# One byte offset and one run length for split weights: the up projection at 192 and 64, the queries and keys at 0 and 8 in runs of sixteen

## The chip, the cores and the metric

The kernel runs on one core of one Trainium2 chip. Five engines with a queue each matter here: TensorE (PE, with its weight loads as PEld), VectorE (DVE), ScalarE (ACT), GpSimd (POOL) and SyncE (SP), whose queue issues the transfers. An engine takes its instructions in the order in which they stand in its queue. The metric is the device time of one execution in microseconds; for a kernel it is the median of its runs.

## The reference

One conditioned decoder layer over 256 tokens of width 2048, in float32, and a last RMSNorm:

```
mod = silu(c) W_ada + b_ada
h   = RMSNorm(x)(1+scale1)+shift1
p   = h W_in        # retention q,k,v,g | HGRN2 q,f,i,g | gates A, B
yA  = W_retO( LN_head(Retention(rope(q),rope(k),v)) * silu(g) )
yB  = W_hgO( RMS_head(HGRN2(silu(q), f, i)) * silu(g) )
x   = x + gate1 * ( (sigmoid(gA)*yA + sigmoid(gB)*yB) W_out )
h2  = RMSNorm(x)(1+scale2)+shift2
u   = causal_depthwise_conv3(h2 W_up) ; [a, b] = split(u)
x   = x + gate2 * ( (silu(a) * b) W_down )
out = RMSNorm_final(x)
```

W_up is 2048 x 11264, W_down 5632 x 2048. The weights are the bulk of the work: each is read once.

## The kernel before

**Split products.** Each product with a weight is made of three: the weight is split into an upper part `wh` (an ACT copy to the type fp32r, L180) and a lower part `wl` (DVE: weight minus `wh`, L185), and the activations likewise into a left and a right half of one tile. With `n` = 256 tokens, an upper part meets both halves and a lower part meets the left one only. Where the weight is the stationary operand, an upper matmul moves 512 columns (both halves at once) and a lower matmul 256; an upper and a lower of one weight block go to the same bank of PSUM.

**Rings.** A weight piece of 128 x 2 x 512 is loaded by SP into a ring of 11 buffers (`raw`), split into a ring of 4 buffers for `wh` and one of 4 for `wl`. `part` (L168 to L171) gives each of these four buffers 64 elements more than a piece needs and lays the piece at a byte offset, the `shift`, inside it. A shift changes the address of the stationary operand and nothing else.

**Stages in order of time.**

1. 16 to 288 us: the input projection's first groups. Four of them (HGRN2's f and q) keep the weight stationary (`mm_cols`, 256 columns a matmul, L225 and L226 upper, L229 lower); after their first pieces these groups are visited in turn, a few row tiles at a time, with the shifts of the group's row in `COLS`; the first pieces have no shift. The others (`mm_rows`, L209, L210, L214) keep the activations stationary.
2. 288 to 387 us: four groups of queries and keys for the retention (`wide_group`). A group has 4 column tiles z, 16 row tiles kt, and 4 steps of 4 row tiles. Each step runs for z = 0, 1 and then for z = 2, 3 (`pair`): 8 upper matmuls (L236), then 8 lower (L239). The first pair sums into the two banks of one PSUM buffer, the second pair into those of another; there are two such buffers (`pg`), and the next group uses the same two. At the end ACT copies the right halves of a buffer to SBUF (L257) and DVE adds the left halves (L258), buffer by buffer. Between the steps the chunk work of HGRN2 is issued (`pump`): scores (L615, L663), the output matmuls `po<-p,at` and `po<-p,a` (L722, L724), their head norm (squares `sqh` L728 and `rsh` L321 on ACT, reciprocal L322 and `oh` L732 on DVE), and the gate f (sigmoid L576, bounds L581 on ACT).
3. 387 to 764 us: gates, values and the output projections by rows.
4. 774 to 1259 us: 22 up groups (`up_group`), 4 column tiles and 16 row tiles each. A step has two row tiles, 8 upper matmuls (L1144) and 8 lower (L1146). `UPS` gives every group a run length and two shifts: with 8 the uppers of a step go first and then its lowers, with 16 two steps are joined, with 2 two uppers and two lowers alternate. Groups alternate between `pg` and four `po` banks, so a group's sums have the length of a group to be emptied.
5. 1259 to 1498 us: the down projection by rows.

**What sets the order.** Instructions that are pinned (`pin`) keep the program's order; the others are placed by a scheduler that looks at engines and buffers. `pump` spends a rate on the work in the background, so a step's `pump` decides at which step the HGRN2 pieces are offered to it.

## Time and profile before

| | us |
|---|---|
| median of 3 runs | 1507.48 |
| lowest and highest | 1507.36, 1507.76 |
| the profiled execution | 1507.86 |
| its span | 1506.0 |
| PE busy | 1489.8 |
| DVE busy | 1207.3 |
| ACT busy | 839.6 |

The profile is of one execution. Its span is the time from the first to the last instruction recorded, 1.9 us less than that execution's own time. A row of a timeline gives the start, the length, the engine, the line of the kernel, the operation, the tiles (out<-in, without buffer numbers), the size, and how many instructions the row joins; in square brackets stands the idle time of the engine just before, and what ended it. Matmuls overlap: the next one starts before the last has ended, so the pace of PE is read from start to start and not from the length of one. Windows give the busy time of each engine in a stretch, and in the column PEclk the clock that PE was granted (1.00 is full).

### The profile page before, as it was taken

The page shows a single profiled execution, that of the slowest core. Times are in us where ns is not written, and L with a number is a line of the kernel's source. Part 1 is how long each engine was busy: PE and PEld are TensorE (multiplying, and loading weights), DVE is VectorE, ACT ScalarE, POOL GpSimd, SP SyncE. Part 2 cuts the span into 40 slices and gives each one's busy share as a digit, 9 for nine tenths or more (in the row PEclk, how much of TensorE's full clock was granted, in tenths as well). Part 3 has the DMA queues.
Part 4 walks back from the last instruction along what each step waited for, and adds up shares of the span by engine and source line. Part 5 has one row for each costly group of instructions (what it writes and reads, how often), then busy time and mean ns, then how long its engine had stood idle before and what let it go on. Part 6 is the DMA issues. An engine that isn't in the chain of part 4 may idle for free.

```text
span 1506.0 us, 22669 instructions
## 1 busy us (share of the span) xinstructions
PE 1489.8 (99%) x8466; PEld 1273.8 (85%) x8466; DVE 1207.3 (80%) x1647; ACT 839.6 (56%) x1210; POOL 4.0 (0%) x8
## 2 busy tenths in 40 slices
PE   8999999999999999999999999999999999999997
PEld 6889899888888888888888888888888888888886
DVE  7899997998999877898977778777777769455694
ACT  5745456767775644455466555545555558344342
POOL 0000000000000000000000000000000000000000
PEclk9999999999999999999999999999999999999999
DMA  9999997878787899989847777777677766667651
GB/s 374 360 340 345 313 335 255 265 253 278 279 277 263 283 302 325 316 292 358 304 129 239 243 231 236 225 238 233 215 248 228 228 188 209 197 207 212 179 186 56
DMA packets 110995, 385.71 MB, mean 256 GB/s; under 512 B 12803, under 2 KB 13347, under 8 KB 110885
## 3 DMA queue, kind: packets, MB, share of 16 engines
q1 hardware_dynamic: 110016, 383.14, 76.7%
q8 instruction: 66, 1.08, 0.3%
q10 hardware_dynamic: 868, 1.13, 0.2%
q14 instruction: 45, 0.36, 0.1%
HBM read 382.11 MB, written 2.11 MB: 255 GB/s over the span
## 4 chain that ended last, share of the span: by engine, by line
PE 94%; DVE 2%; ACT 2%; DMA 1%; issue 1%; SPq 0%; DVEq 0%; ACTq 0%
PE pg L209 13%; PE pg L210 13%; PE pg L214 13%; PE po L1144 11%; PE pg L1144 10%; PE po L1146 5%; PE pg L1146 5%; PE pg L236 4%; PE po L214 3%; PE po L209 3%; PE po L210 3%; PE pg L239 2%; PE pg L229 1%; PE pg L226 1%; PE pg L225 1%; DVE raw L469 1%
## 5 line engine op out<-in xcount | busy, mean ns | idle before, releaser
L185 DVE TENSOR_TENSOR wl<-raw,wh 128x1024 fp32r<-128x1024 f32 (+1 forms) x536 | 631.1, 1189 | 232.6 <-ACT wh L180 194.6
L180 ACT ACTIVATE wh<-raw 128x1024 fp32r<-128x1024 f32 (+1 forms) x536 | 547.3, 1032 | 472.5 <-PE pg L210 198.1
L469 DVE SCALAR_TENSOR_TENSOR raw<-raw,sc 128x1024 f32<-128x1024 f32 x192 | 233.3, 1219 | 0.0
L209 PE MATMUL pg<-wh,hT 128*128 128x512 f32 x512 | 202.2, 395 | 0.7 <-ACT wh L180 0.6
L210 PE MATMUL pg<-wh,hT 128*128 128x512 f32 x512 | 199.8, 390 | 0.0
L1144 PE MATMUL po<-h2T,wh 128*128 128x512 f32 x704 | 178.2, 392 | 0.0
L1144 PE MATMUL pg<-h2T,wh 128*128 128x512 f32 x688 | 173.9, 393 | 0.0
L1144 PEld LDWEIGHTS po<-h2T,wh 128*128 128x128 f32 x704 | 125.0, 188 | 21.3
L1144 PEld LDWEIGHTS pg<-h2T,wh 128*128 128x128 f32 x688 | 122.7, 188 | 21.5
L214 PE MATMUL pg<-wl,hT 128*128 128x512 f32 x512 | 138.4, 390 | 0.1
L209 PEld LDWEIGHTS pg<-wh,hT 128*128 128x128 f32 x512 | 96.1, 188 | 21.1 <-ACT f L590 1.0
L214 PEld LDWEIGHTS pg<-wl,hT 128*128 128x128 f32 x512 | 96.0, 188 | 20.6 <-DVE wl L185 0.4
L210 PEld LDWEIGHTS pg<-wh,hT 128*128 128x128 f32 x512 | 96.2, 188 | 19.6 <-DVE hT L398 0.3
L1146 PEld LDWEIGHTS po<-h2T,wl 128*128 128x128 f32 x704 | 96.3, 188 | 8.5
L1146 PEld LDWEIGHTS pg<-h2T,wl 128*128 128x128 f32 x688 | 93.2, 188 | 8.4 <-DVE wl L185 0.6
L1146 PE MATMUL po<-h2T,wl 128*128 128x256 f32 x704 | 98.2, 279 | 0.0
L1146 PE MATMUL pg<-h2T,wl 128*128 128x256 f32 x688 | 95.3, 279 | 0.1
L210 PE MATMUL pg<-wh,gs 128*128 128x512 f32 x176 | 68.6, 390 | 0.0
L209 PE MATMUL pg<-wh,gs 128*128 128x512 f32 x176 | 68.5, 389 | 0.0
L209 PE MATMUL po<-wh,gs 128*128 128x512 f32 x176 | 68.5, 389 | 0.0
L210 PE MATMUL po<-wh,gs 128*128 128x512 f32 x176 | 68.5, 389 | 0.0
L1157 ACT ACTIVATE u<-uy,convw 128x256 f32<-128x256 f32 x88 | 52.3, 594 | 27.3 <-DVE uy L1155 27.0
(255 smaller groups left out, 2027.9 us busy)
## 6 DMA issues: line engine op xcount, KB each, us to landing
raw<-in_wup SPq DMA_DIRECT2D x176, 512.0 KB, 4.6
raw<-in_wdown SPq DMA_DIRECT2D x88, 512.0 KB, 4.0
raw<-in_wa SPq DMA_DIRECT2D x80, 512.0 KB, 5.7
raw<-in_ada SPq DMA_DIRECT2D x64, 512.5 KB, 5.7
raw<-in_ada SPq DMA_DIRECT2D x64, 512.0 KB, 5.5
raw<-in_wab SPq DMA_DIRECT2D x64, 512.0 KB, 5.2
raw<-in_gate SPq DMA_DIRECT2D x32, 512.5 KB, 5.0
raw<-in_wk SPq DMA_DIRECT2D x32, 512.0 KB, 5.2
```

What stands on the lines that cost most here:

```text
L180: self.pin(self.nc.scalar.activation(wh, raw, AF.Copy))
L185: self.last = self.nc.vector.tensor_tensor(wl, raw, wh.bitcast(F32), ALU.subtract)
L209: nc.tensor.matmul(ps[t], lhsT=act[:, hi], rhs=wh, start=first and i == 0, stop=False)
L210: nc.tensor.matmul(ps[t], lhsT=act[:, lo], rhs=wh, start=False, stop=False)
L214: nc.tensor.matmul(ps[t], lhsT=act[:, hi], rhs=wl, start=False, stop=last and i == len(items) - 1)
L225: nc.tensor.matmul(outs[j], lhsT=wh[:, cs[j]], rhs=act[:, :T], start=opens, stop=False, skip_group_check=True)
L236: nc.tensor.matmul(ps[z], lhsT=wh[:, z * P : (z + 1) * P], rhs=act, start=first and i == 0, stop=False)
L239: nc.tensor.matmul(ps[z][:, :T], lhsT=wl[:, z * P : (z + 1) * P], rhs=act[:, :T], start=False, stop=last and i == len(items) - 1)
L469: dot = self.pin(nc.vector.scalar_tensor_tensor(raw[:, 0, :], raw[:, 0, :], 1.0, self.sc[:, u * GW : u * GW + w], ALU.mult, ALU.mult, accu ...
L1144: self.pin(nc.tensor.matmul(ps[z], lhsT=wh[:, z * P : (z + 1) * P], rhs=act, start=kt == 0, stop=False, skip_group_check=bool(begun)))
L1146: nc.tensor.matmul(ps[z][:, :T], lhsT=wl[:, z * P : (z + 1) * P], rhs=act[:, :T], start=False, stop=kt == KT - 1, skip_group_check=bool(be ...
L1157: nc.scalar.activation(u, y, AF.Identity, bias=w[3], scale=w[2])
```

## The change

The tables go. All four visited column groups take shift 8; before, the third had 72 and the fourth 4. All up groups take runs of eight with the uppers at 192 and the lowers at 64, which two of the 22 groups had before (the second and the nineteenth). The queries and keys take 0 for the uppers and 8 for the lowers (before, (0, 64) and (192, 192) in turn), and a step no longer runs pair by pair: it runs 16 uppers for z = 0 to 3 and then 16 lowers, and offers the background work of two pumps at once behind them. `shift` is now a row of four numbers, two for each of two pieces in turn.

```diff
-UPS = (
-    (2, 192, 192), (8, 192, 64), (8, 192, 192), (16, 144, 64), (8, 192, 8), (8, 192, 208), (8, 192, 176), (8, 192, 0),
-    (8, 192, 224), (8, 176, 64), (8, 208, 64), (8, 200, 64), (8, 184, 64), (8, 224, 64), (16, 144, 8), (16, 144, 192),
-    (16, 192, 8), (16, 144, 0), (8, 192, 64), (8, 192, 192), (16, 144, 64), (2, 192, 192),
-)
-WIDES = ((0, 64), (192, 192), (0, 64), (192, 192))
-COLS = ((8, 8), (8, 8), (72, 72), (4, 4))
+COLS = (8,) * 4
+WIDE = (0, 8, 0, 8)
+UP = (192, 64, 192, 64)
...
-                uppers.append(self.upper(src[:, at : at + z, :], z, G, gain, shift))
+                uppers.append(self.upper(src[:, at : at + z, :], z, G, gain, shift[at % 4 : at % 4 + 2]))
...
-    def mm_wide(self, ps, items, first, last, pair):
+    def mm_wide(self, ps, items, first, last):
 
         nc = self.nc
         for i, (act, wh, _) in enumerate(items):
-            for z in (pair, pair + 1):
+            for z in range(4):
                 nc.tensor.matmul(ps[z], lhsT=wh[:, z * P : (z + 1) * P], rhs=act, start=first and i == 0, stop=False)
         for i, (act, _, wl) in enumerate(items):
-            for z in (pair, pair + 1):
+            for z in range(4):
                 nc.tensor.matmul(ps[z][:, :T], lhsT=wl[:, z * P : (z + 1) * P], rhs=act[:, :T], start=False, stop=last and i == len(items) - 1)
 
-    def wide_group(self, src, act, shift=(0, 0)):
+    def wide_group(self, src, act):
...
-        pieces = self.pieces(src, KT, shift=shift)
+        pieces = self.pieces(src, KT, shift=WIDE)
         for k in steps:
             items = [(act(kt), wh, wl) for _ in range(2) for kt, wh, wl in next(pieces)]
-            for pair in (0, 2):
-                self.mm_wide(ps, items, k == 0, k == steps[-1], pair)
-                self.pump()
+            self.mm_wide(ps, items, k == 0, k == steps[-1])
+            self.pump(2)
...
-            return COLS[cols.index(g)] if g in cols else (0, 0)
+            return COLS if g in cols else (0,) * 4
...
-        run = UPS[i][0]
         for step in pieces:
-            step = list(step)
-            if run == 16 and not begun:
-                step += next(pieces)
             some = [(kt, act2(kt), wh, wl, z) for kt, wh, wl in step for z in range(4)]
-            for at in range(0, len(some), run):
-                part = some[at : at + run]
-                for kt, act, wh, wl, z in part:
-                    self.pin(nc.tensor.matmul(ps[z], lhsT=wh[:, z * P : (z + 1) * P], rhs=act, start=kt == 0, stop=False, skip_group_check=bool(begun)))
-                for kt, act, wh, wl, z in part:
-                    nc.tensor.matmul(ps[z][:, :T], lhsT=wl[:, z * P : (z + 1) * P], rhs=act[:, :T], start=False, stop=kt == KT - 1, skip_group_check=bool(begun))
+            for kt, act, wh, wl, z in some:
+                self.pin(nc.tensor.matmul(ps[z], lhsT=wh[:, z * P : (z + 1) * P], rhs=act, start=kt == 0, stop=False, skip_group_check=bool(begun)))
+            for kt, act, wh, wl, z in some:
+                nc.tensor.matmul(ps[z][:, :T], lhsT=wl[:, z * P : (z + 1) * P], rhs=act[:, :T], start=False, stop=kt == KT - 1, skip_group_check=bool(begun))
             self.pump(len(step) / 2)
```

The number of matmuls and of transfers stays. In the stage of the queries and keys the scheduler places the HGRN2 work differently. The lines of the kernel after stand four to ten lower: the upper matmuls of this stage are L232, the lowers L235, the copy L252, the addition L253.

The first place is on PE, in the third of these groups, around its last step but one. `pg_3519` and `pg_3520` are the group's two buffers, `po_3712` (`po_3693` before) and `po_3730` hold the HGRN2 outputs. Before:

```order
L722 MATMUL po_3693<-p_133,at_3020 128x128 x4
L236 MATMUL pg_3520<-hT_1331,wh_3666 128x512 x4
L236 MATMUL pg_3520<-hT_1658,wh_3672 128x512 x4
L239 MATMUL pg_3520<-hT_1331,wl_3667 128x256 x4
L239 MATMUL pg_3520<-hT_1658,wl_3673 128x256 x4
L722 MATMUL po_3730<-p_133,at_3020 128x128
L724 MATMUL po_3730<-p_133,a_465_3083 128x128
```

And after the change:

```order
L235 MATMUL pg_3520<-hT_1658,wl_3673 128x256 x2
L717 MATMUL po_3712<-p_133,at_3036 128x128 x4
L717 MATMUL po_3730<-p_133,at_3036 128x128
L719 MATMUL po_3730<-p_133,a_465_3099 128x128
L717 MATMUL po_3730<-p_133,at_3036 128x128
```

The four products into `po` that stood between the two pairs of a step now stand behind the whole step, directly ahead of the eight others; after these the group's last step follows in both kernels.

The second place is on ACT, where the copies out of the same group's buffers stand (`p_3805<-pg_3519` and `pg_3520`). Before:

```order
L321 ACT_TABLE_LOAD
L321 ACTIVATE rsh_3704<-ssh_3698,eps_73 128x4
L728 ACTIVATE sqh_3740,ssh_3739<-po_3730 128x128 x4
L490 ACTIVATE gate_2905<-dot_3781 128x1
L321 ACTIVATE rsh_3745<-ssh_3739,eps_73 128x4
L576 ACT_TABLE_LOAD
L576 ACTIVATE f_3785<-p_130 128x1024
L257 ACTIVATE p_3805<-pg_3519 128x512
L581 ACTIVATE f_3785<-f_3785,lb,lb_1687 128x256
L257 ACTIVATE p_3805<-pg_3520 128x512
```

And after the change:

```order
L723 ACTIVATE sqh_3740,ssh_3739<-po_3730 128x128
L571 ACT_TABLE_LOAD
L571 ACTIVATE f_3801<-p_130 128x1024
L723 ACTIVATE sqh_3740,ssh_3739<-po_3730 128x128
L576 ACTIVATE f_3801<-f_3801,lb,lb_1687 128x256
L723 ACTIVATE sqh_3740,ssh_3739<-po_3730 128x128
L576 ACTIVATE f_3801<-f_3801,lb,lb_1687 128x256
L316 ACT_TABLE_LOAD
L316 ACTIVATE rsh_3745<-ssh_3739,eps_73 128x4
L252 ACTIVATE p_3805<-pg_3519 128x512
L252 ACTIVATE p_3805<-pg_3520 128x512
```

The sigmoid of f now stands among the squares instead of behind the second `rsh`, and a table load stands ahead of that `rsh`. The first four squares, another table load and the first `rsh` stand ahead of these rows after the change too: from the first square to the first copy there are three table loads after the change and two before it.

The third place is on DVE, at the end of the fourth group (buffers `pg_3810` and `pg_3811`), where the stage passes into the products by rows. Before:

```order
L185 TENSOR_TENSOR wl_4033<-raw_4030,wh_4032 128x1024
L469 SCALAR_TENSOR_TENSOR raw_4050,dot_4049<-raw_4050,sc 128x1024
L185 TENSOR_TENSOR wl_4058<-raw_4055,wh_4057 128x1024
L609 TENSOR_TENSOR ke_4075<-b_3787 128x512
L258 TENSOR_TENSOR p_4023<-p_4023,pg_3810 128x512
```

And after the change:

```order
L181 TENSOR_TENSOR wl_4058<-raw_4055,wh_4057 128x1024
L181 TENSOR_TENSOR wl_4085<-raw_4082,wh_4084 128x1024
L464 SCALAR_TENSOR_TENSOR raw_4100,dot_4049<-raw_4100,sc 128x1025
L253 TENSOR_TENSOR p_4023<-p_4023,pg_3810 128x512
L253 TENSOR_TENSOR p_4023<-p_4023,pg_3811 128x512
```

The addition out of the first buffer now stands behind one lower split more, that of the third piece of the rows, and behind the dot that follows it; the addition out of the second buffer follows at once.

## The prediction

> **What bounds the kernel now.** I read the page first, then the busy time by stage, then the timeline of each engine at the places where the change acts. The page's head, its line of busy time and the chain of waits by engine:

> ```profile
> span 1506.0 us, 22669 instructions
> PE 1489.8 (99%) x8466; PEld 1273.8 (85%) x8466; DVE 1207.3 (80%) x1647; ACT 839.6 (56%) x1210; POOL 4.0 (0%) x8
> PE 94%; DVE 2%; ACT 2%; DMA 1%; issue 1%; SPq 0%; DVEq 0%; ACTq 0%
> ```

> TensorE (PE) is the chain. The two stages that the change touches most, as windows (start:end, length, then busy PE, PEld, DVE, ACT, POOL, granted clock, DMA share, GB/s): the queries and keys, then the up projection.

> ```profile
> 290.00:390.00 100.00, 99.69 (x919) 87.15 (x918) 94.36 (x131) 67.84 (x106) 1.91 (x2) 1.00 0.83 279
> 793.00:1260.00 467.00, 467.00 (x2694) 409.50 (x2694) 354.18 (x538) 269.70 (x413) 0.00 (x0) 1.00 0.72 227
> ```

> PE waits 0.31 us in the first and never in the second. So time can be won only by matmuls that start at a shorter distance, and it can be lost wherever a wait appears. VectorE (DVE) is 94% busy in the first stage: whatever is late there queues.

> **The up groups.** Group 1 and group 18 already have the new setting (runs of eight, 192, 64). Window rows of group 1, of the twenty groups after it up to the down projection, and of group 18:

> ```profile
> 792.59:814.56 21.97, 21.97 (x130) 19.32 (x129) 16.02 (x24) 13.88 (x19) 0.00 (x0) 1.00 0.74 258
> 814.56:1258.70 444.14, 444.14 (x2563) 389.66 (x2562) 337.20 (x512) 254.93 (x393) 0.00 (x0) 1.00 0.72 226
> 1170.37:1192.34 21.97, 21.97 (x131) 19.32 (x130) 17.40 (x27) 11.99 (x19) 0.00 (x0) 1.00 0.76 246
> ```

> The twenty average 444.14 / 20 = 22.21; both groups with the new setting take 21.97, 378 us apart and beside different DVE and ACT loads. If all get that, the gain is 444.14 − 20 × 21.97 = 4.7 us. Group 0 ran in twos and waited once for a lower part:

> ```profile
> 787.39 0.30 PEld L1146 LDWEIGHTS pg<-h2T,wl 128*128 128x128 f32 x2 [0.56 <-DVE wl L185]
> ```

> With runs of eight the first lower part of a step is wanted eight upper matmuls, about 1.8 us, after the step's first instead of two, so that wait goes: some 0.4 us, and 0.1 for the pace. Up groups together: −5.2.

> [...]

> **The visited column groups.** Two windows of one stage, the first with parts at 8, the second with parts at 72 (60 and 72 matmuls start in them):

> ```profile
> 66.30:73.24 6.94, 6.94 (x61) 6.94 (x60) 4.83 (x9) 6.35 (x10) 0.00 (x0) 1.00 0.86 251
> 73.24:81.76 8.52, 8.52 (x75) 8.52 (x73) 8.52 (x12) 3.71 (x6) 0.00 (x0) 1.00 1.00 355
> ```

> 6.94 / 60 = 115.7 ns against 8.52 / 72 = 118.3 ns. Groups 2 and 3 have 336 visited matmuls that move to 8: 336 × 2.6 = −0.9 us.

> **The pace of queries and keys.** One step of a pair is eight upper (L236) and eight lower (L239) matmuls:

> ```profile
> 291.25 2.00 PE L236 MATMUL pg<-hT,wh 128*128 128x512 f32 x8
> 293.09 1.11 PE L239 MATMUL pg<-hT,wl 128*128 128x256 f32 x8
> 294.03 2.00 PE L236 MATMUL pg<-hT,wh 128*128 128x512 f32 x8
> ```

> From start to start that is 1.84 / 8 = 230 ns an upper and 0.94 / 8 = 117.5 ns a lower. At offset 8 no row shows a lower part of this stage. I bound it by the two 256-column paces above, 115.7 and 118.3, and twice as far to the slow side: 256 lower matmuls give −0.5 to +0.5, the uppers, at 0 as half of them are now, about as much again. I take −0.3, and so −6.4 for all gains.

> **What the order by sixteens costs.** Before, a group's first two banks are complete one pair-step (2.78 us) before its end, so ACT's copy and DVE's addition empty them while the second pair still runs. Now the lower matmuls go z = 0 to 3 per row tile, and the first two banks are complete two or three matmuls before the group ends. All the emptying falls behind the end, and the next group, which reuses these banks, waits for it. The only such wait now is at the third boundary:

> ```profile
> 363.65 1.11 PE L239 MATMUL pg<-hT,wl 128*128 128x256 f32 x8
> 365.07 2.13 PE L236 MATMUL pg<-hT,wh 128*128 128x512 f32 x8 [0.31 <-DVE p L258]
> 363.72 0.58 ACT L257 ACTIVATE p<-pg 128x512 f32<-128x512 f32 x1
> 364.33 0.69 DVE L258 TENSOR_TENSOR p<-p,pg 128x512 f32<-128x512 f32 x1 [0.28 <-ACT p L257]
> 365.42 0.69 DVE L258 TENSOR_TENSOR p<-p,pg 128x512 f32<-128x512 f32 x1 [0.41 <-ACT p L257]
> ```

> It delays PE by 365.07 − (363.65 + 0.94) = 0.48 us. The least a boundary costs is copy plus addition, 0.58 + 0.69 = 1.3 us, less whatever else PE has in its order there. Now boundary by boundary, E being the end of the group's last matmul.

> *Into the first group.* PE's first step now turns to the second pair of banks after seven matmuls (1.6 us from 288.50) instead of waiting for it a pair-step later; DVE empties those banks here, until 290.25:

> ```profile
> 289.04 1.21 DVE L841 TENSOR_TENSOR p<-p,pg 128x1024 f32<-128x1024 f32 x1
> 308.36 1.22 DVE L640 TENSOR_TENSOR e<-b 128x1024 f32<-128x1024 f32 x1
> 384.89 1.22 DVE L185 TENSOR_TENSOR wl<-raw,wh 128x1024 fp32r<-128x1024 f32 x1
> 308.26 0.72 PE L615 MATMUL po<-qe,ke 128*128 128x128 f32 x5
> 338.02 0.74 PE L663 MATMUL po<-eq,kt 128*32 128x16 f32 x64
> ```

> 290.25 − 290.10: +0.2.

> *First to second.* DVE has a lower split ahead of the addition whose buffer only comes free after the first eight lower matmuls of the last step (E − 0.8), then an e (both 1.22 above), so the addition ends at about E + 2.3. PE has 1.35 us of score matmuls in between (the row at 308.26 to the next upper at 309.61). +0.9.

> *Second to third.* Copy and addition, 1.3 us, less 0.67 of scores (338.02 to 338.69): +0.65.

> *Third to fourth.* This is the dear one. Rows of before: the hgrn output matmuls, then ACT's queue, then DVE's.

> ```profile
> 357.25 0.38 PE L722 MATMUL po<-p,at 128*128 128x128 f32 x2
> 358.95 2.08 PE L236 MATMUL pg<-hT,wh 128*128 128x512 f32 x8
> 354.68 0.28 ACT L728 ACTIVATE sqh<-po 128x128 f32<-128x128 f32 x1 [1.70 <-PE po L722]
> 355.08 0.28 ACT L728 ACTIVATE sqh<-po 128x128 f32<-128x128 f32 x1
> 358.02 1.28 ACT L321 ACT_TABLE_LOAD   x1
> 360.97 0.28 ACT L490 ACTIVATE gate<-dot 128x1 f32<-128x1 f32 x1
> 361.15 0.28 ACT L321 ACTIVATE rsh<-ssh,eps 128x4 f32<-128x4 f32 x1
> 361.46 1.28 ACT L576 ACT_TABLE_LOAD   x1
> 362.75 1.06 ACT L576 ACTIVATE f<-p 128x1024 f32<-128x1024 f32 x1
> 365.29 1.58 ACT L581 ACTIVATE f<-f,lb,lb 128x256 f32<-128x256 f32 x3
> 362.92 1.13 DVE L732 SCALAR_TENSOR_TENSOR oh<-po,rsh,p 128x128 f32<-128x128 f32 x4
> ```

> Before, four of the twelve output matmuls ran a pair-step ahead of the others, and ACT reached the copy (363.72) 0.9 us before the group's end. Now all twelve stand just ahead of the last step. That step takes 16 × 0.230 + 16 × 0.1175 = 5.56 us and the last eight of the twelve 1.70 (357.25 to 358.95), so ACT can begin its squares at about E − 7.2. In its new order come, ahead of the copy: eight squares at 0.40 from start to start (3.2), three table loads instead of two at 1.30 (3.9), two rsh at 0.3 (0.6), f at 0.97 to the copy's start, two quarter pieces of f at a third of 1.58 (1.05), a gate (0.2): 9.9 us, so the copies run from E + 2.7 and end at 3.2 and 3.7. DVE cannot start its additions before the second rsh either: the four oh, 1.3 us with their small reciprocal, stand ahead of them from about E + 2.7, so they end at E + 4.7 and E + 5.4. PE starts two uppers (0.46 us) at E + 4.75 and the next at E + 5.4: 4.9 us late where it was 0.48. +4.45. If the oh and the third table load were no hindrance, it would be 1.3 − 0.5 = +0.8; that is the lower bound here.

> *Fourth to the rows.* DVE has a split freed at E − 0.8 (1.22) and a dot of the same length (1.2) ahead of the additions, and PE has nothing:

> ```profile
> 386.35 1.07 PE L239 MATMUL pg<-hT,wl 128*128 128x256 f32 x8
> 387.37 0.50 PE L209 MATMUL pg<-wh,hT 128*128 128x512 f32 x1
> ```

> Now the next matmul follows at once (387.37); then at E + 2.25. Lower bound 1.3.

> Sum of the waits: 0.2 + 0.9 + 0.65 + 4.45 + 2.25 = 8.45. With the gains: +2.05.

> **The clock.** The one stretch at half clock in this trace, a window of 3.41 us, and the one before it:

> ```profile
> 23.23:26.64 3.41, 1.75 (x13) 1.34 (x12) 3.05 (x8) 3.23 (x7) 0.00 (x0) 1.00 1.04 413
> 26.65:30.06 3.41, 3.41 (x17) 3.41 (x18) 3.41 (x6) 1.06 (x1) 0.00 (x0) 0.50 1.03 411
> ```

> A window in which PE idled 1.66 us was followed by one at 0.50, where 17 matmuls fit instead of 3.41 / 0.1157 = 29.5: 12.5 × 0.1157 = 1.5 us lost. A gap of 4.8 us puts at least 2.4 us of idle into one such window, wherever the windows lie, so the third boundary should cost a further 1.5. The gap of 2.25 puts between 1.1 and 2.25 into one; it reaches 1.66 in about two positions in three, and I count it: 1.5 more. Total 2.05 + 3.0 = **+5.1 us**.

> [...]

> **The rivals.**
> *No half clock.* The waits come as worked out, but no window falls to 0.50: +2.05, 1509.5 us, within 0.2%. For it: one row alone carries the price. Against it: that row.
> *Short waits, faster.* ACT and DVE run ahead of PE by so much that each boundary shows only copy and addition: 0.2 + 0 (1.35 of scores cover 1.3) + 0.65 + 0.8 + 1.3 = 2.95, net −3.45, 1504.0 us. It decides if ACT begins the squares 3 us earlier than I think. Against it: their input comes from PE at E − 7.2, and DVE has hardly any idle time.
> *The offsets do nothing.* The pace belongs to the place in the program or to the traffic beside it: 4.7 + 0.9 + 0.3 = 5.9 us of gain fall away, 1512.6 + 5.9 = 1518.5 us. Against it the equal groups 1 and 18; for it, that the other groups also differ by what else runs beside them.

> **How the numbers follow.** The sum was made on the profiled execution (1507.86 us; span 1506.0); against the median of the runs, 1507.48, it gives 1512.6. Chances: forecast 0.57 (one half window rather than two: 1511.1), no half clock 0.23, short waits 0.10, offsets without effect 0.10. The range, 1506.0 to 1517.5, ends between the two lighter rivals and short of the heaviest, and so leaves out most of two cases of 0.10. Measurement tells about 0.2%, 3 us, from no change: slower above 1510.5 (0.65: forecast and last rival, less a tail of the forecast), same 0.25, faster 0.10. The forecast's own range is 1510.5 to 1514.5.

> **What will show it.** Up groups of 21.97 from start to start throughout; 115.7 ns in column groups 2 and 3; a PE gap of about 4.8 us before the fourth group, put down to DVE's addition, with three table loads in ACT's queue ahead of the copy; gaps of 2.2 us before the rows and about 0.9 and 0.65 at the first two boundaries; one or two windows of clock 0.50 after them. I am wrong if the gap at the third boundary is under 2 us, if no window falls to 0.50, or if the up groups stay at 22.2.

## The result and the profile after

| | us |
|---|---|
| before, median of 8 runs | 1507.61 (1507.36 to 1508.38) |
| after, median of 8 runs | 1511.90 (1510.03 to 1512.32) |
| ratio after to before | 1.0026, 95% interval 1.0015 to 1.0037 |
| the profiled execution after | 1512.32, span 1510.5 |

The change costs 4.3 us. The forecast was 1512.6 in a range of 1506.0 to 1517.5. The head of the page after:

```profile
span 1510.5 us, 22666 instructions
PE 1487.1 (98%) x8466; PEld 1271.3 (84%) x8466; DVE 1209.4 (80%) x1647; ACT 839.0 (56%) x1210; POOL 4.0 (0%) x8
PE 93%; DVE 4%; DMA 1%; ACT 1%; issue 1%; SPq 0%; DVEq 0%; ACTq 0%
```

PE is busy 2.7 us less than before and the span is 4.5 us longer: it gained pace and waits more. In the chain of waits DVE's share went from 2% to 4%. The gain is in the up groups. Windows of all twenty-one full groups and of one of them, the seventeenth (start:end, length, busy PE, PEld, DVE, ACT, POOL, granted clock, DMA share, GB/s):

```profile
801.57:1263.01 461.44, 461.44 (x2691) 405.74 (x2689) 354.92 (x537) 267.49 (x411) 0.00 (x0) 1.00 0.73 231
...
1153.14:1175.11 21.97, 21.97 (x130) 19.32 (x129) 17.15 (x28) 12.44 (x20) 0.00 (x0) 1.00 0.77 239
```

461.44 / 21 = 21.97 for every group; before, the same groups took 21.97 + 444.14 = 466.11. The loss is in the queries and keys. PE's timeline at the four boundaries:

```profile
312.64 1.65 PE L232 MATMUL pg<-hT,wh 128*128 128x512 f32 x6 [0.60 <-DVE p L253]
...
339.37 3.92 PE L232 MATMUL pg<-hT,wh 128*128 128x512 f32 x16 [0.57 <-DVE p L253]
...
363.31 2.02 PE L235 MATMUL pg<-hT,wl 128*128 128x256 f32 x16
369.42 5.24 PE L232 MATMUL pg<-hT,wh 128*128 128x512 f32 x16 [4.09 <-DVE p L253]
374.50 2.02 PE L235 MATMUL pg<-hT,wl 128*128 128x256 f32 x16
...
391.10 2.02 PE L235 MATMUL pg<-hT,wl 128*128 128x256 f32 x16
...
395.31 0.51 PE L205 MATMUL pg<-wh,hT 128*128 128x512 f32 x1 [2.19 <-DVE p L253]
```

The second, third and fourth group and the rows behind them now begin with a wait for DVE's addition out of the banks (L253). And behind the longest wait the sixteen uppers take 374.50 − 369.42 = 5.08 us where sixteen take 3.68 elsewhere. What stood ahead of the longest, on ACT and DVE:

```profile
365.81 1.28 ACT L316 ACT_TABLE_LOAD   x1
367.10 0.30 ACT L316 ACTIVATE rsh<-ssh,eps 128x4 f32<-128x4 f32 x1
367.31 1.06 ACT L252 ACTIVATE p<-pg 128x512 f32<-128x512 f32 x2
...
367.64 1.12 DVE L727 SCALAR_TENSOR_TENSOR oh<-po,rsh,p 128x128 f32<-128x128 f32 x4
...
368.69 1.27 DVE L253 TENSOR_TENSOR p<-p,pg 128x512 f32<-128x512 f32 x2
```

The group's last lower matmul began near 365.05, and E, the end of the group, is taken 0.12 us later. ACT was then still busy with HGRN2's queue, and the copies began 2.1 us after E = 365.17, behind the third table load and the `rsh`; DVE did the four `oh` first. That is the chain that the prediction walked through, 0.6 us shorter; ACT's rows, from the third last square at 361.57 to the copies at 367.31, ran in the order listed for its queue under the change.

The clock, in windows laid on the edges that the trace gives for the slow stretches:

```profile
365.43:368.84 3.41, 0.00 (x0) 0.00 (x0) 1.37 (x6) 3.38 (x7) 0.00 (x0) 1.00 0.49 195
368.84:372.25 3.41, 2.83 (x7) 2.28 (x8) 3.05 (x4) 3.41 (x5) 0.00 (x0) 0.50 0.02 5
392.74:396.15 3.41, 1.22 (x8) 0.89 (x7) 3.41 (x6) 3.20 (x4) 0.00 (x0) 1.00 0.91 323
396.15:399.56 3.41, 3.41 (x10) 2.63 (x9) 3.41 (x5) 1.47 (x3) 0.00 (x0) 0.50 0.87 288
```

Both long waits are followed by a window at half clock.

### The profile page after: what moved, and what is told of

The parts are those of the page before. It is cut to its first block, busy times and chain, and to the rows that moved or that the text cites. A ratio compares the mean times of both kernels' runs of the same rounds, so it can differ in the third digit from the quotient of the medians.

```text
span 1510.5 us, 22666 instructions
## 1 busy us (share of the span) xinstructions
PE 1487.1 (98%) x8466; PEld 1271.3 (84%) x8466; DVE 1209.4 (80%) x1647; ACT 839.0 (56%) x1210; POOL 4.0 (0%) x8
## 3 DMA queue, kind: packets, MB, share of 16 engines
q10 hardware_dynamic: 868, 1.13, 0.2%
## 4 chain that ended last, share of the span: by engine, by line
PE 93%; DVE 4%; DMA 1%; ACT 1%; issue 1%; SPq 0%; DVEq 0%; ACTq 0%
PE pg L205 13%; PE pg L210 13%; PE pg L206 13%; PE po L1133 11%; PE pg L1133 10%; PE po L1135 5%; PE pg L1135 5%; PE pg L232 3%; PE po L210 3%; PE po L205 3%; PE po L206 3%; PE pg L235 2%; DVE wl L181 1%; DVE raw L464 1%; PE pg L221 1%; PE pg L222 1%
## 5 line engine op out<-in xcount | busy, mean ns | idle before, releaser
L1135 PE MATMUL po<-h2T,wl 128*128 128x256 f32 x704 | 94.5, 277 | 0.0
L232 PE MATMUL pg<-hT,wh 128*128 128x512 f32 x256 | 64.1, 402 | 5.3 <-DVE p L253 5.3
```

The source lines that it names most:

```text
L232: nc.tensor.matmul(ps[z], lhsT=wh[:, z * P : (z + 1) * P], rhs=act, start=first and i == 0, stop=False)
L1135: nc.tensor.matmul(ps[z][:, :T], lhsT=wl[:, z * P : (z + 1) * P], rhs=act[:, :T], start=False, stop=kt == KT - 1, skip_group_check=bool(be ...
```

## The experiments

The theory on trial: the order by sixteens moves the emptying of the banks behind each group's end; the waits that follow, and the half clock behind the two long ones, cost more than the offsets win. The kernels ran on different chips, so each is compared through its distance to the kernel before on its own chip. The rivals: the offsets 0 and 8, or sixteen matmuls of a kind in a row, are dear in themselves; the offsets win nothing; a slow stretch behind a gap is no matter of the clock.

### Pairs restored

```diff
-            self.mm_wide(ps, items, k == 0, k == steps[-1])
-            self.pump(2)
+            for pair in (0, 2):
+                self.mm_wide(ps, items, k == 0, k == steps[-1], (pair, pair + 1))
+                self.pump()
```

`mm_wide` takes the column tiles as one more argument for this, `zs`, here and in the kernels built on this one.

> The kernel after the change, but the queries and keys run pair by pair again (8 uppers and 8 lowers for z = 0, 1, then for z = 2, 3, one pump behind each pair); the shifts 0 and 8 and all else stay. My theory: the loss sits in the order by sixteens alone, through banks that are emptied behind a group's end, and through the half clock that follows the two long gaps. In the profiles after against before the boundaries cost 0.33 + 0.69 + 0.63 + (4.25 - 0.48) + 2.35 = 7.8 us and the two slow windows 1.4 + 1.7 = 3.1 us. All of it should go: 1511.9 - 10.9 = 1501.0 us, no window at clock 0.50 in this stage, the one wait of about 0.5 us at the third boundary back. Rival, the shifts 0 and 8 or the placement of the HGRN2 pieces cost the time: the stage keeps more than half of its loss, 1507 us or more.

Measured: 1500.89 us (4 runs, 1500.70 to 1501.91), against 1507.07 of the kernel before on the same chip; ratio 0.9961, interval 0.9946 to 0.9976. The only wait for DVE left on PE in this stage is the old one:

```profile
362.93 2.12 PE L232 MATMUL pg<-hT,wh 128*128 128x512 f32 x8 [0.31 <-DVE p L254]
```

So the loss belongs to the order by sixteens together with the `pump` of two behind each step, which this edit takes back as well; the run with pairs in the first and last step, below, tells the two apart. This kernel is faster than both others: the rest of the change is a gain of 6.2 us.

### Sixteens alone

```diff
 # the kernel before, with
-WIDES = ((0, 64), (192, 192), (0, 64), (192, 192))
+WIDES = ((0, 8),) * 4
 # and mm_wide, wide_group with z in range(4) and pump(2) as after the change
```

> The kernel before with one part of the change alone: queries and keys at 0 and 8 in runs of sixteen; the up groups and the column groups keep their tables. My theory: it has the whole loss and none of the gains of the up groups (5.2 us) and of the columns (0.7 us): 1511.9 + 5.9 = 1517.8 us, with the same gaps before the fourth group (4.1 us) and before the rows (2.2 us). Rival, the up groups gained less than their rows say or gave it back elsewhere: 1513 to 1515 us.

Measured: 1515.86 us (4 runs, 1515.52 to 1517.20), ratio 1.0062, interval 1.0045 to 1.0078. That is 8.8 us over the kernel before on its chip, where the forecast stood 10.2 over. The waits are the same (4.08 and 2.19 us). The difference is one slow window. Windows of its trace, on the clock's edges:

```profile
366.39:369.81 3.42, 0.86 (x3) 0.56 (x4) 2.50 (x7) 3.41 (x8) 0.00 (x0) 1.00 0.10 38
369.81:373.22 3.41, 3.41 (x9) 2.64 (x9) 3.37 (x3) 2.90 (x4) 0.00 (x0) 0.50 0.33 70
390.29:393.70 3.41, 2.73 (x20) 2.38 (x18) 1.51 (x2) 2.13 (x4) 0.00 (x0) 1.00 0.87 290
393.70:397.11 3.41, 1.89 (x8) 1.61 (x9) 3.41 (x6) 2.74 (x4) 0.00 (x0) 1.00 0.90 287
397.11:400.53 3.42, 3.42 (x16) 2.82 (x16) 3.42 (x5) 1.48 (x2) 0.00 (x0) 1.00 0.90 325
```

The gap of 2.19 us before the rows lay across an edge here (393.70): 0.68 us of it in one window, 1.52 in the next, and no window fell to 0.50. The same gap lay within one window after the change, and one did. This is where an execution's luck enters: about 1.4 us.

### Pairs in a group's first and last step only

```diff
-            self.mm_wide(ps, items, k == 0, k == steps[-1])
+            for zs in ((0, 1), (2, 3)) if k in (0, steps[-1]) else (range(4),):
+                self.mm_wide(ps, items, k == 0, k == steps[-1], zs)
             self.pump(2)
```

> The kernel after the change, but the first and the last of the four steps of a group of queries and keys run pair by pair; the two middle steps keep the sixteens, and the pump of two stays behind each step. My theory: only the emptying of the banks at a group's end costs, so half of the stage in sixteens is free. The first three small losses (0.33 + 0.69 + 0.63), the wait before the rows (2.35) and the half clock (3.1) go. At the third boundary ACT's queue is still long: the first copy at about E + 0.1, the second, behind a table load and an rsh, with its addition ending at E + 4.65, where PE wants those banks 2.78 us after its start; 1.9 us of wait stay there of 4.25. 1511.9 - 9.5 = 1502.4 us. Rival, sixteen uppers in a row are themselves dear (weight parts wanted sooner, a worse pace): about half of the loss stays, 1506 us or more.

Measured: 1502.20 us (6 runs, 1501.42 to 1502.49), ratio 0.9967, interval 0.9956 to 0.9979; 4.9 us under the kernel before, forecast 5.2. This kernel keeps the `pump` of two, so that is not what cost the time: half of the stage in sixteens is as good as free, and what is dear is the emptying at a group's end. It is 1.3 us over the kernel with pairs. In the two traces the stage, from its first matmul to the first of the rows, is 0.75 us longer (99.57 against 98.82); the remainder lies outside it. The 0.75 us lie at the third boundary, where ACT's queue still has its third table load between the two copies:

```profile
363.94 2.11 PE L232 MATMUL pg<-hT,wh 128*128 128x512 f32 x8 [0.46 <-DVE p L254]
...
367.53 2.12 PE L232 MATMUL pg<-hT,wh 128*128 128x512 f32 x8 [0.54 <-DVE p L254]
...
363.92 1.28 ACT L317 ACT_TABLE_LOAD   x1
```

Two waits, 1.0 us together in the rows where 1.9 us were expected.

### The gaps filled

```diff
+        if fill:
+            idle = self.po()
+            for _ in range(fill):
+                nc.tensor.matmul(idle, lhsT=act(0)[:, :P], rhs=act(0), start=True, stop=True)
         out = self.blk([P, 4, T], name="p")
...
-            begin(self.retention, hb, *[self.wide_group(a["wk"][2 * hb + i], act) for i in range(2)], v.pop(0))
+            begin(self.retention, hb, *[self.wide_group(a["wk"][2 * hb + i], act, (0, 0, 17, 9)[2 * hb + i]) for i in range(2)], v.pop(0))
```

> The kernel after the change with 26 matmuls of 512 columns added that nothing uses: 17 behind the third group of queries and keys, 9 behind the fourth (the scheduler puts two of these nine ahead of the fourth group), each some 0.23 us. They stand where PE waits for the emptying of the banks, so they cost nothing by themselves, and PE is busy. My theory: the clock falls because of the idle time, so both slow windows go: 1511.9 - 3.1 = 1508.8 us, with waits of at most 0.5 us left at these places and no clock under 1.00 there. Rival, the slow stretch behind a gap is no matter of the clock's window but of the weights or of the restart: the time stays at 1511.9 us or rises by what the added matmuls do not hide.

Measured: 1508.44 us (10 runs, 1507.89 to 1509.41), ratio to before 1.0009, interval 0.9999 to 1.0018. It is 1.4 us over the kernel before, where the kernel after the change is 4.3 over: with 26 matmuls more it is 2.9 us faster. The two stretches:

```profile
364.20:372.00 7.80, 7.80 (x37) 6.40 (x37) 4.84 (x10) 7.77 (x14) 0.44 (x1) 1.00 0.31 114
389.00:397.00 8.00, 7.43 (x41) 6.12 (x40) 6.70 (x10) 5.74 (x7) 0.00 (x0) 1.00 0.96 317
```

The clock stays at 1.00, where it was 0.50 from 368.84 and from 396.15 after the change. So the slow stretches come from the idle time. Without them the change would lose 1.4 us in place of 4.3.

### Lower parts at 224

```diff
-UP = (192, 64, 192, 64)
+UP = (192, 224, 192, 224)      # in the kernel with pairs restored
```

> The kernel with the pairs restored (e1), and in all up groups the lower parts at byte 224 instead of 64; nothing else differs, the runs stay eight. My theory: the byte offset of the stationary operand sets the pace, and the ninth group of the kernel before, with (8, 192, 224), took 22.43 us from start to start, so every group now takes 22.43: 1500.9 + 21 x 0.46 + 0.3 for the first = 1510.9 us. Rival, the offsets do nothing and the differences between the groups before came from what else ran beside them: 1500.9 us, groups of 21.97.

Measured: 1506.67 us (10 runs, 1505.48 to 1508.54), ratio to before 0.9995, interval 0.9986 to 1.0004. It is 0.8 us under the kernel before, where the kernel with pairs and 64 is 6.2 under: 5.4 us slower, where 10.0 were expected. The first full group:

```profile
790.06:812.27 22.21, 22.21 (x130) 19.49 (x129) 16.19 (x24) 13.44 (x20) 0.00 (x0) 1.00 0.78 261
```

21 × (22.21 − 21.97) = 5.0 us. The byte alone is worth that, so the rival that the offsets do nothing is out. Nor are the groups' times chance: in the run with sixteens alone, whose up groups keep the table, all 21 full groups repeat the times of the kernel before to 0.01 us. But the size was wrong: the same setting took 22.43 in the kernel before. A group's time does not follow from its setting alone.

### Runs of sixteen in the up groups

```diff
         for step in pieces:
+            step = list(step)
+            if not begun:
+                step += next(pieces)
```

> The kernel with the pairs restored (e1), and in the up groups 1 to 21 two steps joined: sixteen uppers, then sixteen lowers, at the same bytes 192 and 64. My theory: the run length has no price of its own in the up groups, because their banks have a whole group's length to be emptied; in the kernel before, (8, 192, 8) took 22.12 us and (16, 192, 8) 22.13. 1500.9 us, groups of 21.97. Rival, part of the gain of the up groups came from the runs of eight (the table had runs of 16 in six groups, mean 22.25 us): up to 21 x 0.2 = 4 us more, 1505 us.

Measured: 1511.19 us (7 runs, 1510.99 to 1512.63), ratio to before 1.0028, interval 1.0017 to 1.0039; 3.8 us over the kernel before, so 9.9 us slower than with runs of eight. Both the theory and the rival's 4 us missed it. The first and the second full group:

```profile
791.08:813.49 22.41, 22.41 (x131) 19.62 (x130) 15.83 (x24) 13.82 (x21) 0.00 (x0) 1.00 0.70 235
813.49:835.97 22.48, 22.48 (x131) 19.63 (x130) 16.89 (x27) 12.55 (x20) 0.00 (x0) 1.00 0.73 228
```

20 × 0.51 + 0.44 = 10.6 us. There is no wait in these groups; every matmul simply starts later. From start to start the uppers of a group with runs of eight go 226, 229, 232, 226, 229, 232, 226, 236 ns, again and again; with runs of sixteen 233, 233, 234 throughout. The lowers go 113 or 114 ns with a 118 or 119 at the head of each run in the one, 117 to 119 in the other.

### The bytes of the up groups in the queries and keys

```diff
-WIDE = (0, 8, 0, 8)
+WIDE = (192, 64, 192, 64)      # in the kernel with pairs restored
```

> The kernel with the pairs restored (e1), and in the queries and keys the bytes of the up groups, 192 and 64, instead of 0 and 8. My theory: the pace depends on the bytes alone in the same way as in the up groups (uppers 229.4 ns, lowers 114.0), where now an upper takes 232 and a lower 116: 256 x (2.6 + 2) = 1.2 us less, 1499.7 us. Rival, other operands make other favourites there (the first and third group before had 0 and 64 and lowers of 118): no change, 1500.9 us, or a little more.

Measured: 1501.19 us (5 runs, 1500.48 to 1501.68), ratio to before 0.9958, interval 0.9944 to 0.9972; 6.2 us under the kernel before, as with 0 and 8. From the stage's first matmul to its last it takes 98.43 us against 98.70: 0.3 us, not 1.2, and nothing that the times can tell. The rival had the time right, but not the reason. Windows of the first two groups, here and then in the kernel with pairs at 0 and 8:

```profile
286.70:310.48 23.78, 23.78 (x201) 20.95 (x200) 23.04 (x30) 12.15 (x19) 0.00 (x0) 1.00 0.94 325
310.48:335.95 25.47, 25.47 (x306) 21.90 (x304) 25.47 (x33) 16.49 (x28) 0.00 (x0) 1.00 0.71 218
...
286.46:310.41 23.95, 23.95 (x201) 21.10 (x200) 23.11 (x30) 12.22 (x19) 0.00 (x0) 1.00 0.93 316
310.41:335.87 25.46, 25.46 (x306) 21.86 (x305) 25.46 (x33) 16.51 (x28) 0.00 (x0) 1.00 0.74 227
```

In the first group, where HGRN2's matmuls break in only once, near the end, the bytes 192 and 64 do bring the pace of the up groups: 229.5 ns an upper and 114.1 a lower from start to start, against 229.8 and 116.5 with 0 and 8. In the second they break in four times; there, the matmuls beside the breaks left out, the uppers take 231.0 and the lowers 116.6 with either setting. So the same bytes are good here too, but little of the gain is left where other matmuls come between. The theory had also put the uppers before at 232, where the trace has 229.8 to 231.6 by group.

### No shift at all

```diff
-COLS = (8,) * 4
-WIDE = (0, 8, 0, 8)
-UP = (192, 64, 192, 64)
+COLS = (0,) * 4
+WIDE = (0, 0, 0, 0)
+UP = (0, 0, 0, 0)              # in the kernel with pairs restored
```

> The kernel with the pairs restored (e1), and all shifts at 0, in the columns, the queries and keys and the up groups. My theory: the offsets are worth what the rows of the kernel before say of lowers at 0: (8, 192, 0) took 22.35 us against 21.97, at least 21 x 0.38 = 8.0 us, and in the columns some 670 visited matmuls go from 115.7 to about 120 ns, 2.9 us; the queries and keys about 0. 1500.9 + 10.9 = 1511.8 us, with groups of 22.35 us or more. Rival, the offsets do nothing: 1500.9 us.

Measured: 1512.00 us (7 runs, 1511.51 to 1512.83), ratio to before 1.0031, interval 1.0020 to 1.0042. That is 4.6 us over the kernel before, so the offsets together are worth 10.7 us. The up groups took 22.35, as the one with lowers at 0 had taken before, 7.8 us over the 21 groups; the column matmuls took 119.9 ns on the mean in place of 115.7, about 2.9 us for some 680 of them, as expected.

### A probe of the neighbours

```diff
 # the kernel before, with WIDES = ((0, 8),) * 4, COLS = ((8, 8),) * 4 and
+UPS = (
+    (8, 192, 64), (8, 192, 64), (8, 192, 224), (8, 192, 64), (8, 192, 0), (8, 192, 224), (8, 192, 64), (16, 192, 64),
+    (16, 192, 64), (8, 192, 64), (16, 192, 8), (16, 192, 64), (8, 192, 64), (2, 192, 64), (4, 192, 64), (8, 192, 64),
+    (16, 144, 64), (8, 192, 64), (8, 64, 192), (8, 192, 64), (8, 192, 64), (8, 192, 64),
+)
```

> The kernel with pairs, 0 and 8 in the queries and keys and 8 in the columns as in e1, and the up groups as probes, (8, 192, 64) in all but nine. It asks whether a group's pace follows from its own setting or also from the group ahead of it. By the second: (8, 192, 224) takes 22.21 us behind a (8, 192, 64), as in e4, and 22.43 behind a (8, 192, 0), as in the kernel before; the first (16, 192, 64) 22.41 and the second 22.48, as the first and second of e6; (16, 192, 8) about 22.13 and (16, 144, 64) about 22.2. By the first: both (8, 192, 224) the same. In either case the groups with (8, 192, 64) return to 21.97 behind every probe, since they did so behind (2, 192, 192) and (16, 144, 0) in the kernel before; if one does not, the forecast of 4.7 us for the up groups rested on luck with the neighbours. Unknown and without a forecast: runs of 2 and 4 at 192 and 64, and (8, 64, 192). The sum over the run: 1500.9 + some 2.5 to 3.5 us.

Measured: 1505.61 us (8 runs, 1505.24 to 1506.78), ratio to before 0.9987, interval 0.9975 to 0.9998; 2.0 us under the kernel before and so 4.2 over the kernel with pairs, where 2.5 to 3.5 were expected. Windows of eight of its groups, (8, 192, 224), (8, 192, 0), (8, 192, 224), (16, 192, 64) twice, (8, 192, 64) behind them, (4, 192, 64) and (8, 64, 192):

```profile
812.66:834.87 22.21, 22.21 (x130) 19.49 (x129) 17.07 (x26) 12.40 (x20) 0.00 (x0) 1.00 0.74 245
...
856.85:879.13 22.28, 22.28 (x131) 19.52 (x130) 17.06 (x26) 12.48 (x20) 0.00 (x0) 1.00 0.71 224
879.13:901.35 22.22, 22.22 (x130) 19.48 (x129) 17.16 (x26) 12.43 (x20) 0.00 (x0) 1.00 0.73 236
923.33:945.74 22.41, 22.41 (x131) 19.62 (x130) 16.53 (x26) 13.00 (x21) 0.00 (x0) 1.00 0.74 233
945.74:968.22 22.48, 22.48 (x131) 19.62 (x130) 16.89 (x27) 12.55 (x20) 0.00 (x0) 1.00 0.72 217
968.22:990.27 22.05, 22.05 (x130) 19.36 (x129) 17.51 (x27) 12.11 (x19) 0.00 (x0) 1.00 0.74 241
...
1079.06:1101.55 22.49, 22.49 (x131) 19.61 (x129) 16.98 (x26) 12.30 (x19) 0.00 (x0) 1.00 0.74 235
...
1167.85:1190.26 22.41, 22.41 (x130) 19.56 (x129) 16.32 (x26) 12.31 (x20) 0.00 (x0) 1.00 0.73 236
```

Three of the numbers came as expected (22.21 behind a (8, 192, 64); 22.41 and then 22.48). Two things did not. Behind the (8, 192, 0) the group with 224 took 22.22, not 22.43, so that both groups with 224 took the same: by the expectation's own test this pair speaks for the setting alone. But that (8, 192, 0) itself took 22.28 here and 22.35 in the kernel before, so what a group takes over may reach back further than one group; that is argued and not shown. And (8, 192, 64) did not return to 21.97 behind every probe: it needs 22.05 or 22.06 behind each group with runs of sixteen or four, and 22.10 behind the (8, 64, 192), where the kernel before had 21.97 even behind a run of sixteen, (16, 144, 0). Behind the runs of sixteen its first step still goes at 231 to 234 ns an upper, the rhythm of the group ahead, its second is mixed, and from the third on it goes 226, 229, 232; behind the (8, 64, 192) that takes one step more. This costs the neighbour 0.09 to 0.13 us, and the group behind an undisturbed one is at 21.97 again. So a group's pace follows from its own setting plus what it takes over, and (8, 192, 64) finds its rhythm from every start that was tried, within a few steps. Runs of 4 at the same bytes are as dear as runs of 16 (22.49), the two bytes exchanged nearly so (22.41).

## Why the prediction was right, step by step

| step | predicted, us | measured, us |
|---|---|---|
| up groups 1 to 21 | −4.7 | 466.11 to 461.44: −4.7 |
| up group 0 | −0.5 | −0.4 |
| columns and pace of the queries and keys | −1.2 | −1.1 and −0.6 |
| into the first group | +0.2 | +0.3 |
| first to second | +0.9 | +0.7 |
| second to third | +0.65 | +0.6 |
| third to fourth | +4.45 | 4.25 in place of 0.48: +3.8 |
| fourth to the rows | +2.25 | +2.35 |
| half clock, twice | +3.0 | 1.4 and 1.5: +2.9 |
| sum | +5.1 | +4.5 between the profiled executions |

The measured column is read from start to start in the two traces; it sums to +3.9, and the columns' stage began 0.5 us later after the change (66.76 against 66.30), which no step of the working speaks of. Up to the last of the columns' first pieces the two traces are level (33.29 before, 33.25 after), though by different ways: the first column matmul began at 16.76 before and at 18.00 after, a matmul of 256 columns went 213 ns from start to start until 19.7 before and 24.1 after and 120 ns behind that, and the trace before had its slow window at 26.65 besides. The rows that follow began at 33.41 before and, behind a wait of 0.22 us for ACT's copy, at 33.75 after; no run shows whether that belongs to the change. Of the −1.1, 0.9 us are the column matmuls themselves, which went from 117.1 to 115.7 ns on the mean of some 690, as worked out. The waits at the boundaries were worked out from durations in the trace before and the new order of the queues, and each came within 0.25 us except the dearest. There the step "copies run from E + 2.7" was mis-sized: they ran from E + 2.1. ACT began its squares at E − 7.1, as worked out, but its chain took 9.25 us and not 9.9: the eight squares took 2.7 us, not 3.2, because the second four are shorter from start to start (0.25 to 0.37 us) than the 0.40 taken for all, and the two `rsh` took 0.4, not 0.6. The step "no row shows a lower part at 8, I take −0.3" was also too small by half.

The profiled execution had both slow windows. The fastest of the eight runs took 1510.03 us, within 0.5 us of the 1509.5 of the first rival, no half clock; no trace of that run shows which of its windows were slow, so whether the rival came true there stays open. The choice to price the gaps by the one row of the trace before, a window with 1.66 us idle and then one at 0.50, was the step that decided between "slower" and "within 0.2%". The measurement decides for the row: after a window with 1.22 us busy (2.19 idle) the clock was 0.50. That the second slow window came is in part luck: the prediction gave it two positions in three, and in the run with sixteens alone the same gap lay across an edge and cost no half clock.

Where the working was right by luck is the up groups. It took it that a setting has a pace, and gave all groups 21.97 because two had it. The runs with 224 and with sixteens show that a setting's time depends on its run length and on what runs ahead of it, and that some settings have more than one time (22.21 or 22.43). The working held since (8, 192, 64) comes back to its own rhythm from every neighbour, within a few steps, and since behind itself it stays at 21.97. Two samples that agree to 0.01 us behind different neighbours were good evidence for that one setting, though not complete: five of the probe's neighbours add 0.09 to 0.13 us; for 224 there was one sample, and the forecast from it was wrong by 4.6 us.

The rival "the offsets do nothing" is out: the runs with 224 and without shifts differ from the kernel with pairs in nothing but these bytes, and take 5.4 and 10.7 us longer; no run shows which part of the chip the rhythm belongs to, and that stays open.

## What to carry to other kernels

Before making a run of matmuls longer, ask when the banks that it fills are complete and who waits for them: an order that completes half of the banks early, 2.78 us here, hid their emptying but for one wait of 0.31 us in the run with pairs, and it nearly sufficed to keep it in a group's first and last step (1502.20 us against 1500.89). Price a gap on PE at its length plus the window at half clock behind it, some 1.4 us here, when it can lay some 2 us of a window of 3.41 us idle: windows with 2.19 us and more had that price in this case, those with 1.52 and less had not, and between them both happened. And take a byte offset or a run length for matmuls as measured only in the order in which it was measured: try it in all groups before counting on it.

## What the runs showed of the hardware that was not expected

```profile
23.38:26.79 3.41, 1.75 (x12) 1.34 (x12) 3.02 (x7) 3.18 (x7) 0.00 (x0) 1.00 1.04 419
26.79:30.20 3.41, 3.41 (x17) 3.41 (x17) 3.41 (x6) 1.06 (x1) 0.00 (x0) 0.50 1.03 410
...
1491.38:1494.79 3.41, 1.54 (x7) 0.94 (x5) 1.40 (x3) 1.02 (x3) 0.00 (x0) 1.00 0.68 255
1494.79:1498.20 3.41, 0.00 (x0) 0.00 (x0) 1.42 (x4) 0.72 (x1) 0.00 (x0) 1.00 0.57 211
```

So the idle time alone gives no limit. The windows of 1.66 hold matmuls of 256 columns, that of 1.87 matmuls of 512; what decides between them no run shows. The window of 1.66 stands near the program's start, where PE waited 1.45 us for ACT ahead of 25.58 in the trace before; after the change the longest wait from 24.1 to 29 us was 0.34, and no window there was slow.

**A rhythm that is handed on.** In the full up groups, where PE waits for nothing, the uppers of some settings start in a cycle that repeats: 226, 229, 232 ns with (8, 192, 64), 227, 227, 226 with (16, 144, 64) in the kernel before, and 233, 233, 234 with runs of sixteen at 192 and 64. Which cycle it is depended on the bytes of the weights (21.97 us a group at 64, 22.21 at 224), on the run length (22.48 with sixteen), and on the cycle that ran before (22.05 behind a group with runs of sixteen, against 21.97). The spread, 21.97 to 22.49 us a group, is 2.4% of the up projection's time, and nothing in the lists of waits shows it; it is seen only from start to start.
